# A two-layer transformer step on one core: all out, up and down products as 512-column and 256-column steps, and one modulation vector moved from VectorE to TensorE

## The chip, the cores and the metric

The kernel runs on one core of a Trainium2 chip, as one launch. The metric is the device time of that launch in microseconds (us). The engines are called as the profile calls them: PE (TensorE's matmuls), PEld (its weight loads), DVE (VectorE), ACT (ScalarE), POOL (GpSimd) and SP (SyncE, whose queue issues the loads).

## What is computed

The reference is one inference step of a two-layer model on 128 context tokens and 128 latent tokens, both 2048 wide, all in float32. The two sets of tokens use the same weights, so the kernel treats them as 256 columns. Cut to what matters here:

```python
def trunk_layer(x, mod, w_in_l, w_out_l, ...):
    shift1, scale1, gate1, shift2, scale2, gate2 = mod        # six vectors of 2048
    q_r, k_r, v_r, g_r, q_a, k_a, v_a = project(modulate(x, shift1, scale1), w_in_l)
    ...                                                       # retention and attention heads
    x = x + gate1 * (jnp.concatenate([y_r, y_a], axis=-1) @ w_out_l)
    x = x + gate2 * conv_ffn(modulate(x, shift2, scale2), w_up_l, conv_w_l, conv_b_l, w_down_l)
    return x, k_a, v_a, ...

def modulation(cond, w_mod_l, b_mod_l):                       # cond: one vector per set of tokens
    m = jax.nn.silu(cond) @ w_mod_l + b_mod_l                 # 2048 -> 6 * 2048
    return jnp.split(m[..., None, :], N_MOD, axis=-1)

def conv_ffn(h, w_up_l, conv_w_l, conv_b_l, w_down_l):        # 2048 -> 2 * 5632 -> 2048
    up = jnp.pad(h @ w_up_l, ...)
    u = conv_b_l + sum(up[:, j:j + T] * conv_w_l[j] for j in range(CONV_W))
    gate, val = jnp.split(u, 2, axis=-1)
    return (jax.nn.silu(gate) * val) @ w_down_l
```

## The kernel before

**Tiles and pieces.** The weights of the in, out, up and down products are cut into 6144 tiles of 128x128. Eight tiles are a piece (768 pieces, numbered 0 to 767 in the order of work), and a piece is also one load of 512 KB (`raw`). A group is four output columns of 128 rows each, n = 0 to 3; a column needs 16 tiles (12 in the last third of down). Layer 0 has its out product in pieces 88 to 119, up and down in three thirds in pieces 120 to 383; layer 1 has out in 472 to 503 and up and down in 504 to 767. Down's third follows up's third each time.

**Precision.** Each float32 weight tile and each activation is split into a high part (`hi`, rounded to fp32r by ACT, L482) and the rest (`lo`, a subtraction on DVE, L483), by `split_upto`, for the piece three ahead. An activation tile holds both parts side by side, 256 columns each: `hT` for the in and up products, `ypair` (by `Y(kc)`) for out and down. A product is hi x hi + hi x lo + lo x hi. The usual form, `triple`, issues three matmuls of 256 columns (L674 to L676) into one half of a PSUM bank. The other form, under `halves`, issues one matmul of 512 columns with `hi` over both parts and one of 256 columns with `lo` (L614, L616), into a whole bank per column n; when the column is complete, ACT copies the bank's second half (L639, `tb`) and DVE adds it to the first (L640, `r`). Before the change `halves` holds only in layer 1, for up and down from the first down third on. The first two groups of each up product are done as a pair by `duo_piece`, always with `triple`.

**After a column.** `evac` gives the sums of two columns on: for up to `ffn_pair` (conv on ACT and DVE, L778 to L787, then silu and the product, in the three pieces that follow), for out and down to ACT (L758, times the gate, `gx`) and DVE (L760, into `xT`). The last two of the 16 columns of out and of the last down third go by `evac_one` (L732) straight into `xT`; the code calls them single.

**Modulation.** The six vectors of a layer come from w_mod, 16 MB for each vector. They are computed in two ways, listed by tables at the top. DVE dots (`DVESEQ`, `emit_dot`, L415): 128 values per unit, one load of 1 MB (`vec`) and two dots of 2048. PE blocks (`PESEQ`, `QSEQ`, `emit_mod` L406 and `emit_modq` L392): one load of 1 MB and four calls of 512 columns, which the profile lists as eight instructions; four `emit_modq` blocks make a quarter of a vector, which ACT copies (L362) and PE transposes (L447). Vector 5 is gate2, which down's `evac` needs.

**Order.** The order of work is written out by hand as one list of events, and each engine runs its part in that order. A plan spreads the dots over the pieces by their due pieces and by the weights in `DSHARE`; `quota` and `knots` place the pairs of PE blocks. SP issues loads in the order of use, five buffers for `raw` and three for `vec`. Attention, retention and table work stands in `side` tasks; `step_side` takes one step after each piece, and `emit_piece` takes one more in the middle of a piece if more than one task waits:

```python
            if halves(j, g):
                ...
                continue
            ...
            if i == PIECE // 2 - 1 and len(side) > 1:
                step_side()
```

Of the kernel before, what the change touches and what calls it, by code (L numbers as in the profile page):

```python
# [17 lines left out]
KC = D // P  # L18
DEPTH = 2
# [29 lines left out]
def build_work():  # L49
# [51 lines left out]
    for it in items:  # L101
        g = groups[it["g"]]
        key = g["key"]
        for a in range(0, len(it["order"]), PIECE):
# [16 lines left out]
MU = KC * KC // MUNIT  # L121
# [2 lines left out]
PESEQ = [(0, 2), (0, 3)]  # L124

QSTART = [(0, 1 - i // 2, b) for b in range(4) for i in (0, 2)]
QMID = [(1, 2, 1), (1, 2, 2), (1, 2, 3)]
QNORM = {("up", 0): (0, 5, 0), ("kv", 1): (1, 2, 0), ("up", 1): (1, 5, 0)}
QSEQ = QSTART + QMID + list(QNORM.values())
DVESEQ = [(l, v, u) for l, v, n in ((0, 4, 0), (0, 5, 4), (1, 1, 0), (1, 0, 0), (1, 4, 0), (1, 3, 0), (1, 5, 4))  # L130
          for u in range(n, KC)]
DSHARE = {"kv": 0.38, "q": 0.38, "ret": 0.38, "out": 0.42, "up": 0.36, "down": 0.42}


@with_exitstack
def body(ctx: ExitStack, tc: tile.TileContext, io):
# [9 lines left out]
    gstart = {}  # L146
    for j, p in enumerate(pieces):
        g = groups[p["it"]["g"]]
        gstart.setdefault((g["kind"], g["l"]), j)
        g.setdefault("first", j)  # L150

    def mod_event():

# [4 lines left out]
    def dot_event():  # L158

        if issued[1] < len(dots):  # L160
            l, v, u, k = dots[issued[1]]
            events.append(("dot", (l, v, u, k)))
            if (u, k) == (KC - 1, 1):
# [1 line left out]
            issued[1] += 1  # L165

    ahead = 3 * 2 * WIDE
    knots = [(ahead - 5, 0), (gstart["out", 0], 3 * MU // 2), (gstart["up", 0] - 6, 2 * MU), (gstart["kv", 1] + 16, 2 * MU),
             (gstart["out", 1] - 2, 11 * MU // 4)]

    def quota(j, knots):
        if j <= knots[0][0]:
# [10 lines left out]
    for j, p in enumerate(pieces):  # L183
        g = groups[p["it"]["g"]]
# [34 lines left out]
    for j, p in enumerate(pieces):  # L219
        g = groups[p["it"]["g"]]  # L220
# [367 lines left out]
    def emit_piece(j):  # L588
        p = pieces[j]
        it = p["it"]  # L590
        gi = it["g"]
        g = groups[gi]
        if g["parts"] > 1:
            wide_piece(j, p, gi, g)
            return
        if "gb" in it:
            duo_piece(j, p, it)
            return
        if p["first"]:
            cur.clear()  # L600
            cur["ps"] = [None] * 4
            cur["n"] = [0] * 4
        nk = len(it["order"]) // 4
        fin = []
        c = cur["n"]
        for i, (n, kc) in enumerate(p["tiles"]):
            single = g["ns"][n] >= KC - 2 and last_add(g)
            if halves(j, g):
                src = Y(kc) if g["kind"] == "down" else hT[:, kc, :]
                if cur["ps"][n] is None:  # L610
                    cur["ps"][n] = ps_m.tile([P, 512], F32, tag="m", name="acc")
                out = cur["ps"][n]
                c[n] += 1
                nc.tensor.matmul(out, hi_t[j][:, P * i:P * i + P], src, start=c[n] == 1, stop=False,  # L614
                                 skip_group_check=True)
                nc.tensor.matmul(out[:, 0:256], lo_t[j][:, P * i:P * i + P], src[:, 0:256], start=False,  # L616
                                 stop=c[n] == nk, skip_group_check=True)
                if c[n] == nk:
                    fin.append((n, out, single))
                continue  # L620
            b = n if single else n // 2 * 2
            if cur["ps"][b] is None:
                cur["ps"][b] = ps_m.tile([P, 512], F32, tag="m", name="acc")
            out = cur["ps"][b][:, 256 * (n - b):256 * (n - b) + 256]
            c[n] += 1
            src = Y(kc) if g["kind"] in ("out", "down") else hT[:, kc, :]
            triple(out, j, i, src, c[n] == 1 and n == b, c[n] == nk)
            if c[n] == nk and (single or n % 2 == 1):
                fin.append((n, cur["ps"][b], single))
            if i == PIECE // 2 - 1 and len(side) > 1:  # L630
                step_side()
        del hi_t[j], lo_t[j]
        for n, ps, single in fin:
            if halves(j, g):
                if n % 2 == 0:
                    cur["r"] = tp.tile([P, 512], F32, tag="t2", name="r", bufs=4)
                r = cur["r"][:, 256 * (n % 2):256 * (n % 2) + 256]
                t = tp.tile([P, 256], F32, tag="t1", name="tb", bufs=3)
                nc.scalar.copy(t, ps[:, 256:512])  # L639
                nc.vector.tensor_tensor(r, ps[:, 0:256], t, op=ALU.add)  # L640
                if single:
                    evac_one(g, g["ns"][n], r)
                elif n % 2 == 1:
                    evac(gi, g, n, cur["r"])
            elif single:
                evac_one(g, g["ns"][n], ps)
            else:
                evac(gi, g, n, ps)
        run_later()
# [53 lines left out]
    def Y(kc, new=False):  # L703
        if new and kc // 2 not in ytile:
            ytile[kc // 2] = gp.tile([P, 2, 512], F32R, tag="g4", name="ypair")
        return ytile[kc // 2][:, kc % 2, :]
# [9 lines left out]
        later.extend(fresh)  # L716
        fresh.clear()

    def halves(j, g):

        return g["l"] == DEPTH - 1 and g["kind"] in ("up", "down") and g["first"] >= gstart["down", DEPTH - 1]

    def last_add(g):

        return g["kind"] == "out" or g["kind"] == "down" and g["last"]
# [426 lines left out]
```

## Time and profile before

| | before |
|---|---|
| time, median of 3 runs | 2429.84 us (2428.86 to 2434.89) |
| profiled execution: time | 2432.38 us |
| profiled execution: span from first to last instruction | 2430.6 us |
| PE busy | 2371.9 us (98% of the span) |
| DVE busy | 1892.6 us (78%) |
| ACT busy | 1242.9 us (51%) |
| moved by DMA | 619.27 MB, mean 255 GB/s |

The profiled execution is one more run of the same kernel; its time is 1.8 us longer than its span. Busy times count overlapping instructions once. PE's matmuls overlap: one lasts about 0.28 us while the next starts 0.12 us later, so the rate is read from starts, not from durations.

### The profile page before, as it was taken

The numbers are of one execution on the slowest core, as the hardware profiler recorded it, in microseconds if no ns is written. First come the engines' busy times: TensorE is split into PE (matmuls) and PEld (weight loads), VectorE is DVE, ScalarE is ACT, GpSimd is POOL, SyncE is SP. The second block draws the span as 40 slices with busy tenths as digits, with TensorE's granted clock in tenths as the row PEclk, the third lists the DMA queues.
The fourth block names the chain that finished last, engine by engine and source line by source line (L and its number), as shares of the span: only waits on it lengthen the run. The fifth ranks groups of instructions, "written<-read, shape, count | busy, mean of one in ns | idle before, by whom it ended". The sixth has DMA issues, their size and how long they took to land.

```text
span 2430.6 us, 44608 instructions
## 1 busy us (share of the span) xinstructions
PE 2371.9 (98%) x18094; PEld 2204.5 (91%) x18094; DVE 1892.6 (78%) x2565; ACT 1242.9 (51%) x2005; POOL 27.5 (1%) x29
## 2 busy tenths in 40 slices
PE   6999999999999999999999999999999999999997
PEld 3888888899999999999989999999999888888886
DVE  4567777869998899889987787796997567666666
ACT  4534434465544555445556544456555555555555
POOL 0000010000000000000000000000000000000000
PEclk9999999999999999999999999999999999999999
DMA  9988788976787777777775687777675555655553
GB/s 382 351 310 325 277 301 321 354 261 240 282 283 272 252 275 254 275 271 252 264 281 192 245 290 280 289 275 257 231 245 188 190 186 182 190 190 186 190 181 122
DMA packets 146558, 619.27 MB, mean 255 GB/s; under 512 B 16304, under 2 KB 22448, under 8 KB 121392
## 3 DMA queue, kind: packets, MB, share of 16 engines
q1 hardware_dynamic: 138816, 605.24, 70.5%
q10 hardware_dynamic: 7536, 11.19, 1.3%
q8 instruction: 141, 2.31, 0.4%
q14 instruction: 65, 0.53, 0.1%
HBM read 611.64 MB, written 4.72 MB: 254 GB/s over the span
## 4 chain that ended last, share of the span: by engine, by line
PE 87%; DVE 6%; DMA 3%; issue 2%; ACT 2%; SPq 0%; DVEq 0%; POOLq 0%; ACTq 0%; POOL 0%
PE acc L674 20%; PE acc L676 19%; PE acc L675 19%; PE acc L614 15%; PE acc L616 8%; DVE lo L483 2%; PE md L392 2%; DVE hua L415 2%; DMA vec<-in_w_modq 1%; DMA vec<-in_w_mod 1%; PE md L406 1%; ACT hi L482 0%; ACT pr L874 0%; PE aux L902 0%; PE aux L447 0%
## 5 line engine op out<-in xcount | busy, mean ns | idle before, releaser
L483 DVE TENSOR_TENSOR lo<-raw,hi 128x1024 fp32r<-128x1024 f32 x768 | 934.4, 1222 | 245.2 <-ACT hi L482 241.3
L482 ACT CAST hi<-raw 128x1024 fp32r<-128x1024 f32 x768 | 804.0, 1051 | 476.7 <-PE acc L675 354.8
L674 PE MATMUL acc<-hT,hi 128*128 128x256 f32 x3328 | 950.5, 286 | 5.9 <-ACT hT L577 5.9
L676 PE MATMUL acc<-hT,lo 128*128 128x256 f32 x3328 | 931.3, 280 | 2.0 <-DVE lo L483 2.0
L675 PE MATMUL acc<-hT,hi 128*128 128x256 f32 x3328 | 931.8, 280 | 0.6 <-DVE hT L582 0.6
L674 PEld LDWEIGHTS acc<-hT,hi 128*128 128x128 f32 x3328 | 626.9, 188 | 35.4 <-issue 17.0
L675 PEld LDWEIGHTS acc<-hT,hi 128*128 128x128 f32 x3328 | 625.8, 188 | 4.5 <-issue 1.9
L676 PEld LDWEIGHTS acc<-hT,lo 128*128 128x128 f32 x3328 | 627.0, 188 | 3.0 <-DVE lo L483 2.8
L415 DVE SCALAR_TENSOR_TENSOR hua<-vec,cbc 128x2048 bf16<-128x2048 f32 x208 | 475.2, 2285 | 0.7 <-DMA vec<-in_w_dot 0.7
L676 PE MATMUL acc<-ypair,lo 128*128 128x256 f32 x1216 | 344.3, 283 | 2.3 <-DVE lo L483 2.3
L674 PE MATMUL acc<-ypair,hi 128*128 128x256 f32 x1216 | 346.0, 285 | 0.0
L675 PE MATMUL acc<-ypair,hi 128*128 128x256 f32 x1216 | 344.0, 283 | 0.0
L614 PE MATMUL acc<-hT,hi 128*128 128x512 f32 x896 | 316.7, 396 | 0.0
L616 PE MATMUL acc<-hT,lo 128*128 128x256 f32 x896 | 252.7, 282 | 0.0
L614 PE MATMUL acc<-ypair,hi 128*128 128x512 f32 x704 | 247.2, 396 | 0.0
L674 PEld LDWEIGHTS acc<-ypair,hi 128*128 128x128 f32 x1216 | 233.2, 192 | 6.8 <-issue 5.0
L676 PEld LDWEIGHTS acc<-ypair,lo 128*128 128x128 f32 x1216 | 233.2, 192 | 3.0 <-DVE lo L483 3.0
L675 PEld LDWEIGHTS acc<-ypair,hi 128*128 128x128 f32 x1216 | 233.3, 192 | 0.1
L614 PEld LDWEIGHTS acc<-hT,hi 128*128 128x128 f32 x896 | 168.4, 188 | 40.6
L616 PE MATMUL acc<-ypair,lo 128*128 128x256 f32 x704 | 197.5, 281 | 0.0
L616 PEld LDWEIGHTS acc<-hT,lo 128*128 128x128 f32 x896 | 168.3, 188 | 0.0
L614 PEld LDWEIGHTS acc<-ypair,hi 128*128 128x128 f32 x704 | 132.1, 188 | 31.5
(145 smaller groups left out, 1584.2 us busy)
## 6 DMA issues: line engine op xcount, KB each, us to landing
raw<-in_w_up SPq DMA_DIRECT2D x352, 512.0 KB, 4.4
vec<-in_w_dot SPq DMA_DIRECT2D x104, 1024.0 KB, 5.2
raw<-in_w_in SPq DMA_DIRECT2D x176, 512.0 KB, 5.4
raw<-in_w_down SPq DMA_DIRECT2D x176, 512.0 KB, 4.2
vec<-in_w_modq SPq DMA_DIRECT2D x56, 1024.0 KB, 7.2
vec<-in_w_mod SPq DMA_DIRECT2D x32, 1024.0 KB, 8.0
raw<-in_w_out SPq DMA_DIRECT2D x64, 512.0 KB, 5.5
xT<-in_xT ACTq DMA_DIRECT2D x2, 1024.0 KB, 9.9
```

The costliest lines, as they stand in the source:

```text
L392: nc.tensor.matmul(md[0][32 * j:32 * j + 32, :], sc[:, 2 * kc:2 * kc + 32], t[:, 512 * i:512 * i + 512], start=kc < 4, stop=kc >= 12)
L406: nc.tensor.matmul(md[0][32 * j:32 * j + 32, :], sc[:, 2 * u:2 * u + 32], t[:, 512 * j:512 * j + 512], start=u == 0, stop=u == MU - 1)
L415: nc.vector.scalar_tensor_tensor(hua.rearrange("p c t -> p (c t)").bitcast(BF16), raw[key], 1.0, acc[:, k, :], op0=ALU.mult, op1=ALU.mult, ...
L482: nc.scalar.copy(hi, r)
L483: nc.vector.tensor_tensor(lo, r, hi.bitcast(F32), op=ALU.subtract)
L614: nc.tensor.matmul(out, hi_t[j][:, P * i:P * i + P], src, start=c[n] == 1, stop=False, skip_group_check=True)
L616: nc.tensor.matmul(out[:, 0:256], lo_t[j][:, P * i:P * i + P], src[:, 0:256], start=False, stop=c[n] == nk, skip_group_check=True)
L674: nc.tensor.matmul(out, hi, src[:, 0:256], start=first, stop=False, skip_group_check=True)
L675: nc.tensor.matmul(out, hi, src[:, 256:512], start=False, stop=False, skip_group_check=True)
L676: nc.tensor.matmul(out, lo, src[:, 0:256], start=False, stop=last, skip_group_check=True)
```

## The change

All groups of out, up and down, in both layers, now use the form with one 512-column and one 256-column matmul and an addition of the halves, except the two single columns at the end of out and of the last down third, and except the two groups of each up product that `duo_piece` does. In layer 0 the 12 units of vector 5 (gate2) that were DVE dots are computed by PE, as three more quarters of four blocks each; `knots` places them in pairs in pieces 140 to 178, beside the up products. The plan's weights change with it.

```diff
-QMID = [(1, 2, 1), (1, 2, 2), (1, 2, 3)]
+QMID = [(0, 5, 1), (0, 5, 2), (0, 5, 3), (1, 2, 1), (1, 2, 2), (1, 2, 3)]
...
-DVESEQ = [(l, v, u) for l, v, n in ((0, 4, 0), (0, 5, 4), (1, 1, 0), (1, 0, 0), (1, 4, 0), (1, 3, 0), (1, 5, 4))
+DVESEQ = [(l, v, u) for l, v, n in ((0, 4, 0), (1, 1, 0), (1, 0, 0), (1, 4, 0), (1, 3, 0), (1, 5, 4))
           for u in range(n, KC)]
-DSHARE = {"kv": 0.38, "q": 0.38, "ret": 0.38, "out": 0.42, "up": 0.36, "down": 0.42}
+DSHARE = {"kv": 0.42, "q": 0.42, "ret": 0.42, "out": 0.42, "up": 0.34, "down": 0.4}
...
-    knots = [(ahead - 5, 0), (gstart["out", 0], 3 * MU // 2), (gstart["up", 0] - 6, 2 * MU), (gstart["kv", 1] + 16, 2 * MU),
-             (gstart["out", 1] - 2, 11 * MU // 4)]
+    knots = [(ahead - 5, 0), (gstart["out", 0], 3 * MU // 2), (gstart["up", 0] - 6, 2 * MU), (gstart["up", 0] + 12, 2 * MU),
+             (gstart["down", 0] - 6, 11 * MU // 4), (gstart["kv", 1] + 16, 11 * MU // 4), (gstart["out", 1] - 2, 7 * MU // 2)]
...
-            if halves(j, g):
-                src = Y(kc) if g["kind"] == "down" else hT[:, kc, :]
+            if halves(g, n):
+                src = Y(kc) if g["kind"] in ("out", "down") else hT[:, kc, :]
...
-                if single:
-                    evac_one(g, g["ns"][n], r)
-                elif n % 2 == 1:
+                if n % 2 == 1:
                     evac(gi, g, n, cur["r"])
...
-    def halves(j, g):
-
-        return g["l"] == DEPTH - 1 and g["kind"] in ("up", "down") and g["first"] >= gstart["down", DEPTH - 1]
+    def halves(g, n):
+
+        return g["kind"] in ("out", "up", "down") and not (g["ns"][n] >= KC - 2 and last_add(g))
```

Three places show how instructions move. In the changed kernel the lines stand one to three lower: L613 and L615 are L614 and L616 of before, L391 is L392, L414 is L415, L482 is L483, L639 is L640, L671 to L673 are L674 to L676, L984 is L987.

PE in layer 0's up product, at the end of piece 140, before and then after:

```order
L674 MATMUL acc<-hT,hi 128x256
L675 MATMUL acc<-hT,hi 128x256
L676 MATMUL acc<-hT,lo 128x256
L674 MATMUL acc<-hT,hi 128x256
L675 MATMUL acc<-hT,hi 128x256
L676 MATMUL acc<-hT,lo 128x256
```

```order
L613 MATMUL acc<-hT,hi 128x512
L615 MATMUL acc<-hT,lo 128x256
L391 MATMUL md<-vec,sc 32x512 x8
L613 MATMUL acc<-hT,hi 128x512
L615 MATMUL acc<-hT,lo 128x256
```

Two matmuls stand in place of three, and a pair of PE blocks (eight calls) stands between two pieces; the same pair stands at five more places of this product, and behind the second, fourth and sixth of them the four transposes of a quarter.

DVE in the same product, from piece 156 on, before and then after:

```order
L483 TENSOR_TENSOR lo<-raw,hi 128x1024
L792 TENSOR_TENSOR cv<-cv 128x256
L415 SCALAR_TENSOR_TENSOR hua,modT<-vec,cbc 128x2048
L483 TENSOR_TENSOR lo<-raw,hi 128x1024
L799 TENSOR_TENSOR ypair<-cv,ypair 128x256
L415 SCALAR_TENSOR_TENSOR hua,modT<-vec,cbc 128x2048
L483 TENSOR_TENSOR lo<-raw,hi 128x1024 x2
```

```order
L482 TENSOR_TENSOR lo<-raw,hi 128x1024
L789 TENSOR_TENSOR cv<-cv 128x256
L414 SCALAR_TENSOR_TENSOR hua,modT<-vec,cbc 128x2048
L482 TENSOR_TENSOR lo<-raw,hi 128x1024
L639 TENSOR_TENSOR r<-acc,tb 128x256
L796 TENSOR_TENSOR ypair<-cv,ypair 128x256
L482 TENSOR_TENSOR lo<-raw,hi 128x1024 x2
L639 TENSOR_TENSOR r<-acc,tb 128x256
```

An addition of halves (`r`) stands at every second piece. In pieces 144 to 191 there are 22 dots before and 18 after, in the two further up thirds (224 to 287, 320 to 367) 46 before and 42 after.

PE in layer 0's out product, from the last step of the last retention head (its transposes of `ro`, from which the `ypair` of k tiles 6 and 7 is made) to the first matmul that reads that `ypair`; numbers tell tiles apart, `ypair_3672` before and `ypair_3668` after are this tile. Before:

```order
L987 MATMUL aux_4288<-cst_82,ro_4194 128x128 x2
...
L674 MATMUL acc_4112<-ypair_3672,hi_4258 128x256
L675 MATMUL acc_4112<-ypair_3672,hi_4258 128x256
L676 MATMUL acc_4112<-ypair_3672,lo_4259 128x256
L674 MATMUL acc_4112<-ypair_3672,hi_4258 128x256
```

After:

```order
L984 MATMUL aux_4302<-cst_82,ro_4214 128x128 x2
...
L613 MATMUL acc_4108<-ypair_3668,hi_4220 128x512
L615 MATMUL acc_4108<-ypair_3668,lo_4221 128x256
L613 MATMUL acc_4108<-ypair_3668,hi_4220 128x512
L615 MATMUL acc_4108<-ypair_3668,lo_4221 128x256
```

Before, 54 matmuls (18 tiles) stand in the gap; after, four matmuls (2 tiles): pieces in the new form take no step of a side task in their middle, so the head's steps are spread over more pieces.

## Rows read from the trace of the kernel before

**Rows 1.** Page: busy time of each engine, share of the span, instructions.

```profile
PE 2371.9 (98%) x18094; PEld 2204.5 (91%) x18094; DVE 1892.6 (78%) x2565; ACT 1242.9 (51%) x2005; POOL 27.5 (1%) x29
```

**Rows 2.** Waits of PE: waited for, total us, times, longest us.

```profile
PE acc L676 <- DVE lo L483: 4.4, 7, 1.8
```

**Rows 3.** Windows: busy us and instructions of each engine, then PEclk, DMA share, GB/s.

```profile
690.00:778.00 88.00, 88.00 (x736) 88.00 (x735) 78.43 (x78) 41.79 (x65) 0.00 (x0) 1.00 0.82 281
782.00:960.00 178.00, 178.00 (x1514) 178.00 (x1513) 165.77 (x206) 90.89 (x123) 0.00 (x0) 1.00 0.75 262
1590.00:1646.00 56.00, 56.00 (x469) 56.00 (x468) 52.17 (x57) 30.83 (x56) 0.00 (x0) 1.00 0.81 284
1854.00:1940.00 86.00, 86.00 (x489) 74.58 (x488) 50.23 (x59) 44.98 (x76) 0.00 (x0) 1.00 0.57 185
1944.00:2121.00 177.00, 177.00 (x1004) 154.26 (x1003) 123.54 (x183) 100.69 (x155) 0.00 (x0) 1.00 0.59 187
2125.00:2210.00 85.00, 85.00 (x493) 74.95 (x492) 51.15 (x59) 46.32 (x79) 0.00 (x0) 1.00 0.58 191
2349.00:2415.00 66.00, 66.00 (x375) 57.23 (x374) 44.02 (x65) 45.31 (x96) 0.00 (x0) 1.00 0.42 136
```

**Rows 4.** Timeline of PE around a pair of blocks: start, us, instruction.

```profile
1446.24 0.28 PE L676 MATMUL acc<-hT,lo 128*128 128x256 f32 x1
1446.45 1.92 PE L392 MATMUL md<-vec,sc 128*32 128x512 f32 x16
1448.30 0.39 PE L674 MATMUL acc<-hT,hi 128*128 128x256 f32 x1
1448.53 0.28 PE L675 MATMUL acc<-hT,hi 128*128 128x256 f32 x1
```

**Rows 5.** Timeline of PE at a quarter's transposes.

```profile
1489.72 0.60 PE L447 MATMUL aux<-cst,mev 128*128 128x128 f32 x4
1490.16 0.39 PE L939 MATMUL aux<-grp 128*128 128x128 f32 x2
```

**Rows 6.** Timeline of DVE in layer 0's up: one turn of four pieces, a dot inside.

```profile
606.37 0.48 DVE L785 SCALAR_TENSOR_TENSOR cv<-acc,cst,cv 128x254 f32<-128x254 f32 x1
...
609.66 2.29 DVE L415 SCALAR_TENSOR_TENSOR hua<-vec,cbc 128x2048 bf16<-128x2048 f32 x1
...
611.87 1.22 DVE L483 TENSOR_TENSOR lo<-raw,hi 128x1024 fp32r<-128x1024 f32 x1
...
617.83 0.48 DVE L785 SCALAR_TENSOR_TENSOR cv<-acc,cst,cv 128x254 f32<-128x254 f32 x1
```

**Rows 7.** Timeline of DVE in layer 1's up: an addition of halves; what it waited for.

```profile
2308.71 0.42 DVE L640 TENSOR_TENSOR r<-acc,tb 128x256 f32<-128x256 f32 x1 [1.00 <-ACT tb L639]
2309.05 0.48 DVE L785 SCALAR_TENSOR_TENSOR cv<-r,cst,cv 128x254 f32<-128x254 f32 x1
```

**Rows 8.** Groups by line: count, busy us, mean ns, idle us before, releaser.

```profile
L640 DVE TENSOR_TENSOR r<-acc,tb 128x256 f32<-128x256 f32 x104 | 43.8, 424 | 81.4 <-ACT tb L639 81.4
```

**Rows 9.** Timeline of PE: matmuls that waited for DVE, in brackets how long.

```profile
565.52 0.39 PE L676 MATMUL acc<-hT,lo 128*128 128x256 f32 x1 [0.68 <-DVE lo L483]
569.54 0.39 PE L676 MATMUL acc<-hT,lo 128*128 128x256 f32 x1 [0.92 <-DVE lo L483]
1238.53 0.39 PE L676 MATMUL acc<-ypair,lo 128*128 128x256 f32 x1 [1.80 <-DVE lo L483]
```

**Rows 10.** Timeline of DVE in layer 1's last down third: xT behind r.

```profile
2408.82 0.69 DVE L760 TENSOR_TENSOR xT<-gx,xT 128x512 f32<-128x512 f32 x1 [0.76 <-ACT gx L758]
```

**Rows 11.** Timeline of PE and DVE: the last retention head's end, before out needs it.

```profile
404.78 0.38 PE L987 MATMUL aux<-cst,ro 128*128 128x128 f32 x2
407.06 0.43 DVE L799 TENSOR_TENSOR ypair<-ry,ypair 128x256 fp32r<-128x256 f32 x1 [0.47 <-ACT ypair L798]
```

**Rows 12.** Timeline of ACT and DVE behind the last matmul of the last column.

```profile
2415.70 0.37 ACT L639 COPY tb<-acc 128x256 f32<-128x256 f32 x1 [3.81 <-PE acc L616]
2416.57 0.61 DVE L732 SCALAR_TENSOR_TENSOR xT<-r,modT,xT 128x128 f32<-128x128 f32 x2
```

More of the change, by code (lines that the diff above doesn't have):

```diff
@@ L149, in body @@
         gstart.setdefault((g["kind"], g["l"]), j)
-        g.setdefault("first", j)
     def mod_event():
@@ L633, in emit_piece @@
         for n, ps, single in fin:
-            if halves(j, g):
+            if halves(g, n):
                 if n % 2 == 0:
```

## The prediction

> **What bounds the kernel now.** I read the page first: PE is busy for 2371.9 of 2430.6 us [rows 1], so whatever changes the time must change PE's work, its rate, or its few waits. The waits of PE say how little there is to win: beyond the first 60 us, all its waits for `lo` from DVE come to 4.4 us in seven places [rows 2]. The third view is the rate. PE's matmuls overlap, so I take stretches without foreign work from the windows and divide their length by the matmuls that started in them (the count less two, which straddle the edges) [rows 3]. The reader is to see that a tile costs the same in both forms when it reads `hT`, and slightly less in the new form when it reads `ypair`:
>
> - up, three narrow matmuls: 178 / 1512 x 3 = 0.3532 us a tile; new form: 177 / 1002 x 2 = 0.3533.
> - down, three narrow: 88 / 734 x 3 = 0.3597; out, three narrow: 56 / 467 x 3 = 0.3597; down, new form: 86 / 487 x 2 = 0.3532, 85 / 491 x 2 = 0.3462, 66 / 373 x 2 = 0.3539.
>
> [...] The new form only loads `hi` once instead of twice. That shows in the weight loads, busy for 178 of 178 us before and 154.26 of 177 us in the new form, and not in the time: the loads were hidden already.
>
> **The rate, tile by tile.** Newly in the new form are 448 tiles of out (28 columns of 16), 680 of down in layer 0 (256 + 256 + 192, less 24 single ones), 1280 of up in layer 0 and 384 in layer 1's first third: 2768. The 1664 of up gain nothing, 0.3532 against 0.3533. The 1128 that read `ypair` gain between 0.3597 - 0.3539 and 0.3597 - 0.3462, so 6.5 to 15.2 us; I take the mean of the three measured rates, 0.3511: **-9.7 us**. The 24 single tiles of layer 1's last down go back to three narrow ones, at most 24 x 0.0135 = 0.3: **+0.2**.
>
> [...]
>
> **The vector moved to PE.** Twelve blocks come to PE in six pairs. A pair, between two pieces of the same kind, holds the next tile back from 0.12 to 2.06 us behind the last matmul (1446.24 to 1448.30), and the matmul after that starts 0.23 instead of 0.12 us later: 1.94 + 0.11 = 2.05 us [rows 4]; six are **+12.3**. Three quarters need transposes, 0.44 us each [rows 5]: **+1.3**. Their loads replace the twelve loads of the dots and stand in SP's queue some five to eight pieces ahead of use, so I count no wait for them; SP waits for PE's release of a `vec` buffer and holds the `raw` loads behind it, which have a lead of four to five pieces.
>
> **DVE.** It loses 24 dots and gains 176 additions. A dot holds it 611.87 - 609.66 = 2.21 us [rows 6], so 53 us go; an addition, back to back, takes 0.34 us [rows 7], so 60 come. Where they fall matters. In layer 0's up a turn of four pieces with two dots takes 617.83 - 606.37 = 11.46 us [rows 6], against 32 x 0.3532 = 11.30 on PE. After the change there are 1.5 dots and two additions in a turn: 11.46 - 1.11 + 0.68 = 11.03. DVE still fits, by 0.27 us in 11.3, and PE hides it, with `lo` up to three pieces (8.5 us) ahead. If that cover went, each us that DVE lacks in a turn would be one of PE's.
>
> - At 565 and 569 us PE waited 0.68 and 0.92 us [rows 9] behind the four conv steps of the first two up groups and dots beside them. Until piece 144 the dots there become four instead of six, and a pair of PE blocks gives DVE time: **-1.6** (0 if the additions take the room).
> - In layer 0's last down DVE builds the next layer's tables beside six dots; PE's longest wait, 1.80 us at 1238 [rows 9], is there, and the dots stay six. Added are two additions for two columns, and a gap: `gx` now reads `r`, so DVE stands 0.76 us between `r` and `xT` [rows 10], which it cannot fill, since it works in order. That is 1.44 us for three pieces, 5.3 us over the eleven pieces where it is behind. Some of it meets slack before and behind: **+3.0** (0 to 5.3).
> - Layer 0's out loses the side steps in the middle of pieces. The last head's `ypair` is now needed two tiles, 0.71 us, behind its transposes instead of 18; from the transposes to its last write took 407.06 + 0.43 - 404.78 = 2.7 us with DVE busy between [rows 11], and about 1.9 without. PE waits 1 to 2 us there; up to 3 if a dot or a `lo` stands before: **+1.5** (0.5 to 3).
>
> **The end.** The last column is single and again goes straight from PSUM: `xT` starts when `tb` started, 2416.57 - 2415.70 = 0.87 us sooner [rows 12]: **-0.9**.
>
> **Sum.** -9.7 + 0.2 + 12.3 + 1.3 - 1.6 + 3.0 + 1.5 - 0.9 = **+6.1 us**. On the profiled execution that is 2432.38 + 6.1 = 2438.5 us; it ran 2.5 us above the median of the runs, so for a median I forecast 2429.84 + 6.1 = 2435.9, **2436 us**, 0.25% more. With every bound low (-15.2, -2.1 with the refill of PE, 0, 0.5) the sum is -3.9, with every one high (-6.5, 0, 5.3, 3) +14.7: 2426 to 2444.5.
>
> **Rivals.**
>
> - *The rate of up falls too.* Down's three stretches in one form ran at 0.3462 and 0.3535, so the rate settles at one of several values. If up's 1664 tiles settled at 0.3462, they would give 1664 x 0.0070 = 11.7 us, and the forecast is 2424; with `ypair` at 0.3462 throughout 5.5 more, 2419, faster. Against it: two up thirds in the new form show 0.3533 (one of them here) and no stretch of up anything else.
> - *DVE becomes the bound in up.* An addition needs the column's last matmul, and DVE waits in order: in layer 1 it stood 81.4 us before 104 of them, 0.78 us each [rows 8]. There it had nothing to catch up; with dots it has. If each addition cost 0.34 + 0.78, a turn would take 11.03 + 1.56 = 12.6 us, 1.3 more than PE, in some 50 turns with dots: +65 us, 2500. It decides once DVE reaches an addition early and the next dots then use up the lead, 8.5 us less the 5.9 us of an addition, four conv steps, a dot and a `lo`. Since standing early means that it is ahead, I expect little of it; a third of it would be 2455. This is the case on the slower side.
> - *A wide step costs less than two narrow ones.* If it cost as much as one, 2768 x 0.1177 = 326 us would go, 2110. The windows speak against it in three stretches of down and one of up. [...]
>
> **How the numbers follow.** The forecast has 0.72, the falling rate 0.09, DVE as the bound 0.16, the cheap wide step 0.01, the rest 0.02. Within 0.3% (7.3 us, about what these runs can tell from no change) is 2422.5 to 2437.1. The forecast's own range, 2426 to 2444.5, straddles the upper bound: 0.47 of its 0.72 below, 0.23 above, 0.02 for faster. The falling rate adds 0.05 to faster and 0.04 to same, DVE 0.15 to slower and 0.01 to same, the rest is split. So faster 0.09, same 0.52, slower 0.39. The range reaches 2423 to 2450: it takes in the lesser half of the falling rate and the beginning of DVE as the bound.
>
> **What would show it.** Right: up in layer 0 at 0.353 us a tile with about two thirds of the matmuls; out and down at 0.346 to 0.354; six gaps of 2.05 us between pieces 140 and 178; no waits for `lo` at 565; some 5 us of waits in layer 0's last down; one wait for `ypair` near 410 us. Wrong: waits for `lo` spread over the up thirds with dots, a rate of up below 0.350 or above 0.356, or waits of the moved blocks for their loads.

## The result, and the profile after

The changed kernel took 2469.38 us (median of 4 runs, 2468.90 to 2469.55) against 2432.36 us of the kernel before on the same chip: 1.015 times as long [1.0134, 1.0166]. The forecast was 2436 us, range 2423 to 2450; the time lies 19 us above the range. The profiled execution took 2469.55 us, with a span of 2467.8 us.

The page and the waits of PE answer to [rows 1] and [rows 2]. Page of the changed kernel (busy us, share of the span, instructions):

```profile
PE 2385.7 (97%) x15434; PEld 2077.8 (84%) x15434; DVE 1901.8 (77%) x2698; ACT 1303.6 (53%) x2184; POOL 26.4 (1%) x29
```

Its waits of PE (total us, times, longest us):

```profile
PE aux L886 <- ACT pr L871: 9.7, 4, 3.4
PE acc L615 <- DVE lo L482: 7.2, 10, 2.2
PE aux L984 <- ACT ra L942: 6.0, 4, 2.1
...
PE aux L965 <- DVE rk L951: 5.6, 4, 2.0
PE acc L613 <- DVE ypair L796: 4.4, 2, 2.9
```

The same three side steps in the kernel before (L889 is L886 there, L987 is L984, L968 is L965):

```profile
PE aux L889 <- ACT pr L874: 3.2, 4, 1.5
PE aux L968 <- DVE rk L954: 2.8, 3, 2.0
PE aux L987 <- ACT ra L945: 2.3, 3, 1.4
```

PE has 2660 matmuls fewer and is busy 14 us longer: the six pairs of blocks came. But three of the five waits shown are not of the products that were edited. L886 transposes attention probabilities, L965 and L984 belong to the retention heads: they are side steps of the *in* products, where the diff changes only weights of the plan. They waited 8.3 us before and wait 21.3 us now.

To see where the time went I cut both traces into stages, each from the start of its first product matmul to that of the next stage; the first one begins and the last one ends with the span. Before in us, the other columns as differences to it (labels are those of the experiments below):

| stage | before | after | `move_only` | `halves_only` | `dots_kept` | `dots_kept_last_down_old` | `last_down_clear` |
|---|---|---|---|---|---|---|---|
| layer 0 in, pieces 0 to 47 | 208.5 | +4.8 | +1.2 | +4.5 | +1.1 | +1.5 | -0.5 |
| layer 0 in, pieces 48 to 87 | 180.2 | +11.4 | +8.3 | +1.2 | -0.6 | +1.2 | -0.3 |
| layer 0 out | 114.0 | +1.3 | -1.1 | +2.9 | +1.4 | +1.4 | +3.0 |
| layer 0 up, third 1 | 185.5 | +11.2 | +9.8 | +4.4 | +9.1 | +9.1 | +20.5 |
| layer 0 down, thirds 1 and 2 | 184.4 | -3.4 | 0.0 | +1.8 | -3.6 | -3.8 | -2.3 |
| layer 0 up, thirds 2 and 3 | 316.6 | 0.0 | 0.0 | +0.5 | 0.0 | 0.0 | 0.0 |
| layer 0 last down | 79.7 | +10.7 | +0.5 | +13.5 | +12.2 | +2.5 | -5.3 |
| layer 1 in | 298.5 | +6.0 | +8.1 | +1.5 | +1.6 | +2.0 | +2.0 |
| layer 1 out and up, third 1 | 284.5 | -0.7 | 0.0 | +7.7 | +0.7 | +2.6 | -0.3 |
| the rest | 578.6 | -4.1 | -3.5 | -4.1 | -4.1 | -0.5 | -0.7 |

One execution of each stands here. Stages that an experiment didn't edit still move by 1 to 4 us (the first row and the last above all), so the argument rests on larger differences, and one of that size is no more than a hint.

Forecast were +12 for the first up third and +3 for the last down, and nothing for the in products. The up third came as forecast; the last down cost 10.7, and the in products 17.4 us (pieces 48 to 87, and layer 1).

**The rates** answer to [rows 3]. Windows of the changed kernel in layer 0's out, first down, second up and second down third, and layer 1's out:

```profile
456.00:476.00 20.00, 20.00 (x116) 17.06 (x119) 18.16 (x22) 9.92 (x19) 0.00 (x0) 1.00 0.90 337
...
722.00:805.00 83.00, 82.88 (x472) 71.99 (x472) 73.36 (x83) 44.12 (x75) 0.00 (x0) 1.00 0.74 261
813.00:985.00 172.00, 172.00 (x976) 149.70 (x975) 162.87 (x222) 97.15 (x150) 0.00 (x0) 1.00 0.74 254
994.00:1076.00 82.00, 82.00 (x465) 70.97 (x464) 72.77 (x83) 43.74 (x74) 0.00 (x0) 1.00 0.74 260
1614.00:1640.00 26.00, 26.00 (x153) 22.99 (x152) 22.06 (x35) 12.42 (x25) 1.57 (x1) 1.00 0.77 280
```

With the same division as in the prediction a tile takes 0.351, 0.353, 0.353, 0.354 and 0.344 us: what reads `ypair` gains, up does not.

**The in products.** DVE of the kernel before, at the first query group of layer 0's in product: two dots (L415), the rotation (L827) and the maximum over the scores (L866):

```profile
221.32 2.29 DVE L415 SCALAR_TENSOR_TENSOR hua<-vec,cbc 128x2048 bf16<-128x2048 f32 x1
...
225.27 2.28 DVE L415 SCALAR_TENSOR_TENSOR hua<-vec,cbc 128x2048 bf16<-128x2048 f32 x1
...
230.46 0.69 DVE L827 TENSOR_TENSOR rt<-aux,cst 128x512 f32<-128x512 f32 x1 [0.17 <-PE aux L825]
234.18 0.69 DVE L866 TENSOR_REDUCE st<-aux 128x4 f32<-128x512 f32 x1
```

PE's scores there, and its transposes of the probabilities that follow from them:

```profile
233.09 1.05 PE L860 MATMUL aux<-KT,grp 128*128 128x128 f32 x8
...
241.37 0.63 PE L889 MATMUL aux<-cst,pr 128*128 128x128 f32 x4 [0.86 <-ACT pr L874]
```

The same place in the changed kernel (lines three lower, L414 for the dot):

```profile
229.34 2.29 DVE L414 SCALAR_TENSOR_TENSOR hua<-vec,cbc 128x2048 bf16<-128x2048 f32 x1 [1.09 <-DMA vec<-in_w_dot]
...
233.30 0.68 DVE L824 TENSOR_TENSOR rt<-aux,cst 128x512 f32<-128x512 f32 x1
235.22 2.29 DVE L414 SCALAR_TENSOR_TENSOR hua<-vec,cbc 128x2048 bf16<-128x2048 f32 x1
...
239.17 0.68 DVE L863 TENSOR_REDUCE st<-aux 128x4 f32<-128x512 f32 x1
```

```profile
235.60 1.05 PE L857 MATMUL aux<-KT,grp 128*128 128x128 f32 x8
...
246.34 1.09 PE L886 MATMUL aux<-cst,pr 128*128 128x128 f32 x4 [3.16 <-ACT pr L871]
```

The plan spreads the dots that are left by new weights, and the pairs of vector 4 move from pieces 45, 50, 55, 60 to 46, 51, 56, 62 and so on. Before, both dots are done ahead of the rotation; after, one stands ahead of it and one behind, ahead of the scores. So before, the maximum starts as the scores are done (233.09 + 1.05 = 234.14 us); after, DVE goes without a gap from that dot to a `lo` (237.43 us), a sum (238.57) and the maximum (239.17), which so starts 2.5 us behind the scores (235.60 + 1.05 = 236.65), ACT's exponentials come behind it, and PE waits 3.16 us for 0.86. (The 5 us between the two starts of the maximum are for the most part the 4.8 us that the stage itself begins later.)

In the two in stages together all of PE's waits above 0.15 us came to 15.6 us before and 25.0 after: 9.4 of the 17.4 us. The likely rest is half clock, of which 20.4 us lie in these two stages (next paragraph).

**The clock.** In such waits, or just behind them, the granted clock fell. Windows of the changed kernel before and behind that wait, behind one of 2.48 us at 290 and one of 3.44 us at 1380 us (PEclk is the third number from the end):

```profile
237.00:243.10 6.10, 6.10 (x50) 5.86 (x48) 3.46 (x9) 2.58 (x10) 0.00 (x0) 1.00 1.01 420
246.40:252.10 5.70, 5.70 (x25) 2.39 (x26) 3.29 (x5) 2.37 (x3) 0.00 (x0) 0.50 0.54 175
...
293.20:296.50 3.30, 3.30 (x15) 3.12 (x15) 2.91 (x4) 1.79 (x3) 0.00 (x0) 0.50 0.01 2
...
1383.20:1388.60 5.40, 5.40 (x22) 5.04 (x23) 4.14 (x7) 3.43 (x7) 0.00 (x0) 0.50 0.69 229
```

PEclk 0.50 is what "half clock" means here; ahead of the first of these waits it was 1.00. Between 60 us and the tail such stretches cover 34.0 us of the changed kernel, in eight places, and 3.4 us before, in one.

**The last down.** DVE of the changed kernel there, dots and `lo`, and PE behind it:

```profile
1247.50 2.28 DVE L414 SCALAR_TENSOR_TENSOR hua<-vec,cbc 128x2048 bf16<-128x2048 f32 x1
...
1249.71 1.22 DVE L482 TENSOR_TENSOR lo<-raw,hi 128x1024 fp32r<-128x1024 f32 x1
...
1261.91 2.29 DVE L414 SCALAR_TENSOR_TENSOR hua<-vec,cbc 128x2048 bf16<-128x2048 f32 x1
...
1264.12 1.22 DVE L482 TENSOR_TENSOR lo<-raw,hi 128x1024 fp32r<-128x1024 f32 x1
```

```profile
1250.99 0.38 PE L615 MATMUL acc<-ypair,lo 128*128 128x256 f32 x1 [1.31 <-DVE lo L482]
...
1265.40 0.39 PE L615 MATMUL acc<-ypair,lo 128*128 128x256 f32 x1 [2.17 <-DVE lo L482]
```

Each `lo` starts within 0.1 us of the dot's end, and PE's two longest waits for `lo` in this stage end as it ends. The `hi` that the first of them needs had been ready for 6 us:

```profile
1242.29 1.05 ACT L481 CAST hi<-raw 128x1024 fp32r<-128x1024 f32 x1
```

So the `lo` at 1249.71 us took its turn behind the dot. The stage's longest wait of all, 2.90 us before the first matmul that reads the last `ypair` (1229.62 us), ends with that `ypair` too, which stands on DVE behind two dots, at 1222.12 and 1225.81 us.

### The profile page after: what moved, and what is told of

Same layout as the page of the kernel before. It is cut to its first block, busy times and chain, and to the rows that moved or that the text cites. A ratio compares the mean times of both kernels' runs of the same rounds, so it can differ in the third digit from the quotient of the medians.

```text
span 2467.8 us, 39588 instructions
## 1 busy us (share of the span) xinstructions
PE 2385.7 (97%) x15434; PEld 2077.8 (84%) x15434; DVE 1901.8 (77%) x2698; ACT 1303.6 (53%) x2184; POOL 26.4 (1%) x29
## 4 chain that ended last, share of the span: by engine, by line
PE 82%; DVE 9%; DMA 4%; issue 2%; ACT 2%; DVEq 0%; ACTq 0%; POOLq 0%; SPq 0%
PE acc L613 37%; PE acc L615 19%; PE acc L671 7%; PE acc L672 7%; PE acc L673 7%; DVE lo L482 3%; DVE hua L414 3%; PE md L391 2%; DMA vec<-in_w_modq 2%; PE md L405 1%; DMA vec<-in_w_mod 1%; DMA raw<-in_w_in 1%; ACT hi L481 1%; ACT gx L755 0%; DVE grp L665 0%
## 5 line engine op out<-in xcount | busy, mean ns | idle before, releaser
L482 DVE TENSOR_TENSOR lo<-raw,hi 128x1024 fp32r<-128x1024 f32 x768 | 935.3, 1222 | 240.7 <-ACT hi L481 222.3
L613 PE MATMUL acc<-hT,hi 128*128 128x512 f32 x2560 | 902.4, 395 | 0.0
L615 PE MATMUL acc<-hT,lo 128*128 128x256 f32 x2560 | 720.6, 281 | 1.4 <-DVE lo L482 1.4
L613 PE MATMUL acc<-ypair,hi 128*128 128x512 f32 x1808 | 638.7, 398 | 4.4 <-DVE ypair L796 4.4
L613 PEld LDWEIGHTS acc<-hT,hi 128*128 128x128 f32 x2560 | 481.2, 188 | 119.2 <-ACT ypair L795 1.7
L615 PE MATMUL acc<-ypair,lo 128*128 128x256 f32 x1808 | 507.8, 281 | 6.1 <-DVE lo L482 5.9
L671 PE MATMUL acc<-hT,hi 128*128 128x256 f32 x1664 | 487.5, 293 | 5.9 <-ACT hT L576 5.9
L615 PEld LDWEIGHTS acc<-hT,lo 128*128 128x128 f32 x2560 | 480.3, 188 | 2.0 <-DVE lo L482 2.0
L672 PE MATMUL acc<-hT,hi 128*128 128x256 f32 x1664 | 468.9, 282 | 0.4 <-DVE hT L581 0.4
L673 PE MATMUL acc<-hT,lo 128*128 128x256 f32 x1664 | 468.3, 281 | 0.0
L414 DVE SCALAR_TENSOR_TENSOR hua<-vec,cbc 128x2048 bf16<-128x2048 f32 x184 | 420.4, 2285 | 1.1 <-DMA vec<-in_w_dot 1.1
L613 PEld LDWEIGHTS acc<-ypair,hi 128*128 128x128 f32 x1808 | 340.1, 188 | 90.4 <-DVE ypair L796 5.1
L615 PEld LDWEIGHTS acc<-ypair,lo 128*128 128x128 f32 x1808 | 341.7, 189 | 10.1 <-DVE lo L482 9.8
L671 PEld LDWEIGHTS acc<-hT,hi 128*128 128x128 f32 x1664 | 316.7, 190 | 36.1 <-issue 18.8
L672 PEld LDWEIGHTS acc<-hT,hi 128*128 128x128 f32 x1664 | 316.3, 190 | 4.2 <-issue 1.9
L673 PEld LDWEIGHTS acc<-hT,lo 128*128 128x128 f32 x1664 | 316.6, 190 | 0.0
L638 ACT COPY tb<-acc 128x256 f32<-128x256 f32 x280 | 103.8, 372 | 355.8 <-PE acc L615 351.0
L639 DVE TENSOR_TENSOR r<-acc,tb 128x256 f32<-128x256 f32 x280 | 117.1, 421 | 94.7 <-ACT tb L638 94.0
L755 ACT ACTIVATE gx<-r,modT 128x128 f32<-128x128 f32 x240 | 79.5, 396 | 57.6 <-DVE r L639 57.2
L775 ACT ACTIVATE cv<-r,cst 128x256 f32<-128x256 f32 x160 | 89.2, 598 | 19.4 <-DVE r L639 19.2
L391 PE MATMUL md<-vec,sc 128*32 128x512 f32 x544 | 73.7, 650 | 23.2 <-DMA vec<-in_w_modq 12.0
```

The costliest lines, as they stand in the source:

```text
L391: nc.tensor.matmul(md[0][32 * j:32 * j + 32, :], sc[:, 2 * kc:2 * kc + 32], t[:, 512 * i:512 * i + 512], start=kc < 4, stop=kc >= 12)
L414: nc.vector.scalar_tensor_tensor(hua.rearrange("p c t -> p (c t)").bitcast(BF16), raw[key], 1.0, acc[:, k, :], op0=ALU.mult, op1=ALU.mult, ...
L482: nc.vector.tensor_tensor(lo, r, hi.bitcast(F32), op=ALU.subtract)
L671: nc.tensor.matmul(out, hi, src[:, 0:256], start=first, stop=False, skip_group_check=True)
L672: nc.tensor.matmul(out, hi, src[:, 256:512], start=False, stop=False, skip_group_check=True)
L673: nc.tensor.matmul(out, lo, src[:, 0:256], start=False, stop=last, skip_group_check=True)
```

## The experiments

**Theory:** the dots, put elsewhere by the plan, meet the side steps of the in products, and the dots in the last down meet additions; waits follow, and half clock behind them. **Rivals:** the blocks that came to PE are the whole loss; or the additions make DVE the bound all over.

The first four ran against 2431.66 us of the kernel before (7 runs).

**1. `halves_only`: the new form alone.** The changed kernel with the tables, weights and knots of before (cut):

```diff
-QMID = [(0, 5, 1), (0, 5, 2), (0, 5, 3), (1, 2, 1), (1, 2, 2), (1, 2, 3)]
+QMID = [(1, 2, 1), (1, 2, 2), (1, 2, 3)]
...
-DSHARE = {"kv": 0.42, "q": 0.42, "ret": 0.42, "out": 0.42, "up": 0.34, "down": 0.4}
+DSHARE = {"kv": 0.38, "q": 0.38, "ret": 0.38, "out": 0.42, "up": 0.36, "down": 0.42}
```

> The new form for all out, up and down products, but the vector stays on DVE and every dot stands where it stood before. If additions make DVE late only where it was full already: nothing is lost in layer 0's in product (219 to 405 us of the changed kernel), the first up third loses up to 11 us (8 dots in 16 pieces and two additions in a turn of four pieces: 12.14 us of DVE against 11.30 of PE), layer 0's last down about 10 us as in the changed kernel, and the rate of out and down gives some 5 us back: 16 us above before, 2447. If the moved vector's PE blocks were the whole loss: about 5 us below before, 2425. If the additions made DVE the bound in every up third with dots: 60 us above, 2490.

Measured: 2466.32 us (2457.94 to 2470.58), ratio 1.0137 [1.0111, 1.0163]. Its longest wait row but for the start:

```profile
PE acc L615 <- DVE lo L482: 22.7, 31, 2.8
```

No vector moved, and the form alone costs nearly as much as the whole change, far more than the 2447 that I expected. So the blocks on PE are not the whole loss. The in products are quiet here (+1.2, +1.5), but for the +4.5 of the first row, which is open; the loss is 13.5 us in the last down and 17.3 us in out, up and the first down thirds. Of the waits for `lo`, 8.1 us stand in the last down and 14.5 in those other stages, where dots and additions meet. It is of the kind of the prediction's rival "DVE becomes the bound in up", but up itself shows little of its +65: 4.4 us in the first third, 0.5 in the other two.

**2. `move_only`: the tables alone.** The kernel before with the tables, weights and knots of the change, its form kept; the diff of `halves_only` the other way round, on the kernel before:

```diff
-DSHARE = {"kv": 0.38, "q": 0.38, "ret": 0.38, "out": 0.42, "up": 0.36, "down": 0.42}
+DSHARE = {"kv": 0.42, "q": 0.42, "ret": 0.42, "out": 0.42, "up": 0.34, "down": 0.4}
```

> The vector moves to PE and the dots take the places of the changed kernel, but the form of the products stays as before. If the dots' new places in the in products cost PE waits and the lower clock: 12 us for the six pairs and the transposes net of the waits at 565 us, 11 in layer 0's in product, 6 in layer 1's, up to 4 at the start: 25 to 35 us above before, 2457 to 2467, and no more than before in layer 0's last down. If only the new form's additions cost: 12 us above before, 2444.

Measured: 2458.78 us (2455.79 to 2461.80), 1.0111 [1.0096, 1.0126].

```profile
PE aux L889 <- ACT pr L874: 9.4, 4, 3.4
```

The wait of the changed kernel is there, without one new addition of halves (L889 is L886 there). The in products lose 8.3 and 8.1 us, the first up third 9.8. As the theory of places says.

**3. `dots_kept`: the changed kernel with the in products' dots at their old pieces.** Only the plan is edited (`KEEP` lists the pieces of before; up to piece 112 it takes in layer 0's out as well, less one pair of dots):

```diff
+    for j in range(len(plan)):
+        if j < 113 or 384 <= j < 472:
+            plan[j] = int(j in KEEP)
```

> The changed kernel, with the dots of both layers' in products (pieces 0 to 112 and 384 to 471) in the pieces where they stood before; all else as changed. If their places make the waits of PE for attention and retention there, and these the lower clock: 15 to 20 us below the changed kernel, 2450 to 2454, with the in products as long as before. If the new form or the PE blocks make them: 2469, unchanged.

Measured: 2449.37 us (2448.35 to 2456.26), 1.0078 [1.0062, 1.0095]: 20.0 us less than the changed kernel, nothing else edited (the kernel before differed by 0.7 us between the two measurements).

```profile
PE aux L895 <- ACT pr L880: 3.6, 5, 1.6
```

The long waits for probabilities are gone (L895 is L886 there), the in products stand at -0.6 and +1.6: 12.0 and 4.4 us came back there, 3.7 in the first row, and layer 0's out moved by 0.1. This settles the largest part.

**4. `dots_kept_last_down_old`:** the same, with layer 0's last down in the old form.

```diff
     def halves(g, n):
 
+        if g["kind"] == "down" and g["last"] and g["l"] == 0:
+            return False
```

> As dots_kept, and layer 0's last down third in the old form, without additions. If the additions and the wait of xT behind r make DVE late there: 7 to 11 us below dots_kept, some 2443. If the table work and the dots alone make it late: no more than 2 us below dots_kept.

Measured: 2445.56 us (2439.78 to 2451.80), 1.0057 [1.0035, 1.0079]. The stage gave back 9.7 us as expected; the medians differ by 3.8 us only, and the runs overlap. The profile shows 8 us lost again in stages that were not edited. So the stage is settled, its whole worth in the time is not.

Of the other six, 5, 7, 8 and 9 ran against 2430.42 us (21 runs), 6 and 10 against 2431.90 us (15 runs).

**5. `waits_filled`: work put into the waits.** In the changed kernel, ahead of the probability transposes, into their tile:

```diff
+            if (l, g, j) in ((0, 0, 0), (0, 1, 1), (1, 0, 1)):
+                for _ in range(8):
+                    nc.tensor.matmul(ps, hT[:, 0, 0:P], hT[:, 0, :], start=True, stop=True)
```

> The changed kernel, with eight 512-column steps (into the tile that the next four transposes overwrite, so nothing of the result changes) put ahead of the three probability transposes that waited longest for ScalarE (3.16, 2.48 and 3.44 us at 243, 290 and 1380 us of the changed kernel's trace). At 0.236 us a step they fill 1.9 us of each wait, which stays as long as it was. Theory that a wait lowers TensorE's clock behind it: the half-clock stretches at 245.3 (6.8 us), 293.1 (3.4 us) and 1381.9 (6.8 us) are gone, and half of their 17.0 us comes back: 2461 (2459 to 2464), against 2469.4 of the changed kernel. Rival, that the clock falls there for another reason (the narrow fp32 transposes and products of this stretch): the stretches stay, 2469 to 2471.

Measured: 2472.62 us (2467.76 to 2474.07), 1.0169 [1.0155, 1.0183]. A miss by its making: two of the three sets stood behind the wait themselves, since ACT still read the tile they write, and the half clock behind them stayed (at 287.4 and 1379.7 us); at the third the wait was filled, no half clock came, and its stage went from +3.8 to +1.5 us. So by itself it says little of the time.

**6. `waits_filled_apart`:** the same into a tile of the products' pool, which nobody reads.

> The changed kernel again with eight 512-column steps ahead of the same three probability transposes, now into a tile of the products' own pool, so that they need not wait for the tile that ScalarE still reads; what they compute is thrown away, and the result is unchanged. Two of the three sets stood behind the wait in the version waits_filled, where the stretches at half clock stayed (287.4 and 1379.7 us); the third filled its wait, the stage went from +3.8 to +1.5 us, and no half clock was there. Theory that the wait is what lowers the clock: near 246, 290 and 1380 us no half clock is left, the three stages give back 7 us (4 to 9), 2462 (2460 to 2465) against 2469.4. Rival, that the clock falls for what TensorE does there: half clock stays at 290 and 1380 us, 2468 to 2471.

Measured: 2465.39 us (2459.88 to 2470.84), 1.0147 [1.0130, 1.0164]. Windows behind the three places:

```profile
242.80:248.00 5.20, 5.20 (x39) 3.25 (x39) 3.59 (x6) 2.23 (x3) 0.00 (x0) 1.00 0.52 154
...
292.20:296.00 3.80, 3.80 (x30) 3.69 (x31) 2.95 (x5) 1.52 (x3) 0.00 (x0) 1.00 0.92 351
...
1371.10:1378.00 6.90, 5.93 (x46) 5.62 (x47) 5.69 (x9) 4.60 (x9) 0.00 (x0) 1.00 0.67 229
```

PEclk is 1.00 at all three, for 0.50 there in the changed kernel, with the same transposes and products behind: by these windows the wait had lowered it, not the work. The two in stages gave back 3.1 and 2.3 us, the median 4.0, less than the 7 expected; the interval of the time does not exclude the rival's 2468, the windows do, in one execution. My estimate for the 17.0 us at PEclk 0.50 (experiment 5) was half of their length, 8.5 us. The runs gave back less, 5.4 in the two stages. Part of the slow work may have stood beside waits that came anyway (1.56 us are left at 1369 us); that is not shown.

**7. `last_down_clear`: `dots_kept`, with the ten dots of pieces 356 to 377 (`LATE`) moved ahead**, eight of them into the first up third (`EARLY`).

```diff
+    for j in EARLY:
+        plan[j] += 1
+    for j in LATE:
+        plan[j] -= 1
```

> The version with the dots of the in products at their old places, and beside it the ten dots of pieces 356 to 377 (layer 0's last down and the two pieces before it) moved to pieces 142 to 166 and 294, where VectorE has 90% of its time taken. Theory that the dots, 2.29 us each ahead of the lo part that TensorE waits for, make the last down late: that stage falls from 92.0 us by 6 to 9 us, to the 80 to 84 us of the old form and below, and the time from 2449.4 to 2441 to 2444. Rival, that the longer way of a sum (copy by ScalarE, addition of halves, gate by ScalarE, addition to x, each waiting for the one before on VectorE's queue) makes it late whatever the dots do: the stage stays above 88 us, and the time is 2446 to 2450. Third: the dots take the room in layer 0's first up third, where the pairs of PE stand: 2449 or more.

Measured: 2446.97 us (2444.60 to 2448.69), 1.0066 [1.0052, 1.0080]. The last down fell by 17.5 us, twice what was expected, to 5.3 below before: in the new form without dots it is the fastest of all. But the first up third grew by 11.4, and the time lies above the 2441 to 2444 that I expected. In that up third PE waited 2.7 us for `lo` in three places, and a pair of blocks waited for its load, with half clock around it (6.8 us from 620 us on; PEclk 0.53 in the window from 622 to 627):

```profile
621.73 1.93 PE L407 MATMUL md<-vec,sc 128*32 128x512 f32 x8 [3.95 <-DMA vec<-in_w_modq]
```

Both the theory and its third case came in kind. It takes dots and additions together to make the last down late: dots without new additions cost 0.5 and 2.5 us there (experiments 2 and 4), additions without dots -5.3, both 12.2. Where the dots went, blocks waited for their load; dots and blocks share the three `vec` buffers, and that these were held too long is my reading, not shown.

**8. `one_pair_moved`: the kernel before, one dot from piece 50 to piece 52.**

```diff
+    plan[50], plan[52] = 0, 1
```

> The kernel before, with a single dot moved: the pair that stands at pieces 50 and 51 stands at 51 and 52, as in the changed plan. Theory that such a place costs by itself, since the dot then stands ahead of the rotation and the scores of the first query group on VectorE: the transposes of the probabilities near 240 us wait 3 us longer than the 0 to 0.5 us of before, half clock follows, and the stage from 213 to 251 us takes 3 to 5 us more, the rest nothing: 2435.5 (2434.5 to 2437). Rival, that it takes the whole moved plan: within 0.5 us of 2431.7.

Measured: 2432.35 us (2428.14 to 2436.60, 11 runs), 1.0004 [0.9994, 1.0014]: no change.

```profile
244.48 1.09 PE L891 MATMUL aux<-cst,pr 128*128 128x128 f32 x4 [4.09 <-ACT pr L876]
```

The wait came (4.09 us, for 0.86 at this place before), the four transposes behind it took 1.09 us for 0.63, as they did at half clock in the changed kernel (246.34 us), and the group of pieces 54 to 61 took 3.4 us more. But the group of pieces 50 and 51, out of which the dot went, took 2.7 less. I had not counted that; this one place is worth about nothing in the time, as the rival had it, and the loss needs the run of places.

**9. `halves_where_room`: the kernel before, with the new form only in layer 0's first two down thirds**, and two of sixteen pairs of dots there moved to the up thirds behind, which keep the old form (a list places the dots of pieces 184 to 359; it is left out here).

```diff
+        if g["kind"] == "down" and g["l"] == 0 and not g["last"]:
+            return True
```

> The kernel before, its vectors and tables as they were, with the new form in the first two down thirds of layer 0 alone, and two of their sixteen pairs of dots moved into the up thirds behind them, which keep the old form. What the versions with the changed tables showed there is -1.9 and -1.5 us at 7 pairs of dots in a third. Theory that the form pays where VectorE has room: those two stages fall by 3.4 us together, no other stage moves by more than 0.5, and the time is 2428 (2426.5 to 2429.5) against 2431.7. Rival, that VectorE is late beside the additions even so (as where the additions met 16 dots a third, +1.8 and 0.0): 2431 to 2434. Rival two, that the moved pairs make the old up late: +1 to +3 in the second and third up third, 2429 to 2432.

Measured: 2426.49 us (2423.63 to 2431.15, 11 runs), 0.9985 [0.9977, 0.9994]: 3.9 us less than before, the one version that beats both. The two stages fell by 2.0 of the 3.4 us expected, with seven pairs of dots left in each. The profile shows a further 7.5 us less in two up thirds that were not edited (the first of each layer, in part at a faster rate, see the end), and 4.5 more in the in product of layer 0, so the time is measured, its place only in part.

**10. `halves_all_down`:** that, with the last down in the new form too, and two pairs of its dots left; the others stand in the two up thirds ahead (the list is left out again; the new condition holds for all of layer 0's down).

```diff
-        if g["kind"] == "down" and g["l"] == 0 and not g["last"]:
+        if g["kind"] == "down" and g["l"] == 0 and g["c0"] >= 0:
```

> The version halves_where_room (2426.5) with layer 0's last down in the new form too, and all but two pairs of the dots of that stage moved to the second and third up thirds, which keep the old form (16 and 12 pairs of dots there, where before has 13 and 10). Theory that the last down was late by the dots: with no dots at all it took 74.6 us where before has 79.8, so with two pairs 75 to 78, and 2422 to 2425 in all. Rival, that VectorE has no room left in the old up thirds at a pair in four pieces (before ran its first third so without a loss, at 98% of VectorE's time): those two stages lose more than the last down gains, 2427 to 2435.

Measured: 2433.82 us (2429.37 to 2438.95, 11 runs), 1.0013 [1.0004, 1.0022]. Neither case as put: the denser up thirds lost nothing, but the last down still took 3.7 us more than before.

```profile
1213.07 0.39 PE L622 MATMUL acc<-ypair,lo 128*128 128x256 f32 x1 [1.99 <-DVE lo L489]
1235.36 0.39 PE L622 MATMUL acc<-ypair,lo 128*128 128x256 f32 x1 [1.84 <-DVE lo L489]
```

Each wait ends with a `lo` that stood behind a dot (dots at 1209.59 and 1231.88 us): in this stage two pairs are too many in the new form, none makes it the faster one.

## Why the prediction was wrong

- **The failed step** is the sentence that DVE "loses 24 dots and gains 176 additions" and "where they fall matters". I followed it through up, last down and out, the products that the diff edits, and took the in products for untouched, at 0. The plan places all dots anew from its weights, and there they met the side steps: 17.4 us in the two in stages by the trace, 20.0 us of time given back by experiment 3, 16.4 of it in these stages. The order of the changed kernel would have shown it.
- **Half clock behind waits** was in no term. I priced a wait at its length; where the clock fell behind, it cost more, some 5 us for three waits (experiment 6).
- **The last down:** the mechanism was right, the size was not: +10.7 for +3.0. I priced the gap in front of `xT` by the piece. What counts is a dot ahead of the `lo` or `ypair` that PE needs next, 1.3 to 2.9 us for the three longest waits, with the additions beside (experiments 4, 7 and 10).
- **The rate, -9.7:** right in kind, mis-sized in effect. Layer 0's first two down thirds gave 3.4 us where my rate gives 512 x 0.0086 = 4.4. Out gave none of its 3.9: layer 0's out lost 1.3 and layer 1's gained 0.4, with the wait for `ypair` and small waits for `lo` in between. The last down's 168 tiles drowned in waits.
- **The blocks on PE, +12.3, the transposes, +1.3, and -1.6 at the first up groups** were right: together 12.0, measured 11.2. A pair still holds the next tile back by about 2 us: in the changed kernel 628.71 to 630.77.

```profile
628.71 0.28 PE L615 MATMUL acc<-hT,lo 128*128 128x256 f32 x1
628.92 1.92 PE L391 MATMUL md<-vec,sc 128*32 128x512 f32 x16
630.77 0.50 PE L613 MATMUL acc<-hT,hi 128*128 128x512 f32 x1
```

- **Layer 0's out, +1.5:** right; PE waited 1.53 us for that `ypair` at 427 us. **The end, -0.9:** right, 14.0 us from the last product to the end of the span for 14.9 [rows 12].
- **The rivals:** up's rate did not fall (0.353 us a tile), and a wide step cost two narrow ones: from 899.81 to 901.93 us of the changed kernel's trace the next matmul starts 0.235 us behind the start of a 512-column one and 0.118 behind that of a 256-column one. DVE as the bound did not come in up: the second and third up thirds took as long as before, with additions beside the 42 dots that were left there. With no dot moved, up lost 4.4 us in its first third (experiment 1), far from +65. The two halves of the change do not add up, 34.7 us and 27.1 alone (experiments 1 and 2), 37.0 together: the move also takes dots from stages that get additions. My chance of 0.39 for slower stood beside a range that reached 2450, and what happened was none of the cases.

Left open: the +4.8 us of the first stage. PE waited 2.75 us there at 71 us for a load of a block, with half clock behind; its first product matmul started at 38.3 us for 33.9. But in `dots_kept`, where that start was at 38.9, the stage shows +1.1, and in `move_only` +1.2, so it may be one execution's. Of the -4.1 us of the last row only the end, -0.9, is explained.

## What to carry to other kernels

When a change takes work out of a planner's hands, the planner moves the work that is left: compare the order in the stages that the diff does not touch first, and price a long instruction by what stands behind it on its engine: here dots of 2.28 and 2.29 us, each ahead of a `lo`, made PE wait 1.31 and 2.17 us. Additions of halves paid here where DVE had room for them beside its dots (3.9 us less in experiment 9); beside the dots and table work of the last down the stage was 12.2 us longer than before (`dots_kept`): put the new form where the trace shows such room, and leave it out elsewhere. The version that beat both kept seven of eight pairs of dots in each of the two down thirds that it changed; in the last down, with table work beside, two pairs were already too many. A wait of PE is to be priced above its length where half clock has followed such waits in the trace, as in the eight places of the changed kernel.

## What the runs showed of the hardware

- In the changed kernel half clock followed waits of 3.16, 2.48, 2.14, 2.17, 2.75 and 3.44 us and two of 1.57 and 1.58, but not one of 2.90 at 1227 us, nor those of 1.99 at 367 us, 1.90 at 1449 us and another of 1.57 at 1709 us. Which waits are followed I can't say from these rows.
- The same tiles ran at one of a few rates over a whole stretch: 0.353 or 0.360 us in three narrow matmuls, 0.344 to 0.354 in the new form. In the kernel of experiment 8, with nothing edited there, four groups of layer 1's up took 0.9 us less each than in the trace of before: 21.76 us for 64 tiles in place of 22.61, 0.340 us a tile in three narrow matmuls. What sets the rate is not shown.
